# Loading the merge's first rows and weights under the last attention values, and moving a tile's last block behind its other blocks

## The chip, the cores and the metric

The kernel runs on one core of a Trainium2 chip. The metric is the device time of one execution in microseconds (us); a lower time is better. The time shown is the median of three runs; a profile is one further execution.

## What is computed

One layer on 1024 tokens of width 1024, all in float32. A projection of x feeds a short convolution, an attention with three branches (compressed, selected and window) and two gates; the two paths are merged, projected and normalised, and a mixture of 32 experts follows.

```python
y_a = (b_gate * conv) @ w_up_conv
o_nsa = nsa_attention(...)                     # 1024 x 512
y_b = o_nsa @ w_up_nsa                         # 1024 x 1024
merged = sigmoid(mg_a) * y_a + sigmoid(mg_b) * y_b
x1 = layer_norm(DN_ALPHA * x + merged @ w_o, ln1_g, ln1_b)
x2 = layer_norm(DN_ALPHA * x1 + moe_ffn(x1, ...), ln2_g, ln2_b)
```

The change touches the lines of `y_b`, `merged` and `merged @ w_o`.

## The kernel before

**Numbers.** TensorE multiplies in a float32 form of reduced width. So each operand is split into a high part (a cast on ScalarE) and a low part (what is left, a subtraction on VectorE): `split`, lines 110 to 113. A product is three matmuls, high by high, high by low and low by high: `mm3`, lines 116 to 120. Weights too are loaded as float32 and split in this way.

**Order of the work.** The program is written as one sequence for all engines. A scheduler places each engine's instructions, each engine runs its own in the order it was given, and waits are on semaphores. SyncE's queue issues most loads and writes in its order, so an issue that waits holds up those behind it.

**Attention** (`attention`, lines 549 to 708). The work is cut into 16 units: 8 tiles of 128 tokens, and two groups of heads each. `scores(u)` multiplies queries and keys (`s`, L595 and L596), takes the minimum on VectorE (L597) and the exponential on ScalarE (L599). `values(u)` scales the probabilities, transposes them in steps of 128 keys (`t`, L645), splits them (`th`, `tl`, two steps in flight through the two buffers of `t`), and multiplies them into `o` (L638, "flush"). At the end `o` is copied and added (`otmp` L659, `of` L660 and L661) and written to `o_d[0]` (first 512 tokens) or `o_d[1]` (second 512, L662). The values of one unit run beside the scores of the next, so the last unit's values run alone.

**The late projection** (`late`, lines 664 to 685). The gates of the second 512 tokens are projected under the attention: 16 groups of 8 steps, each step one `mm3` from the operands `x[0]` and `x[1]` (tiles `x10`, `x11`) and weights `lw` into `lm`, followed by a tanh `tg` (L680) and a write to `spill` (L684). How fast its 128 steps are handed out beside the scores is a line in `passed`, the work of the scores so far:

```python
while made < 16 * KT * (passed / total * LATE[0] - LATE[1]):   # L696
```

With `LATE = (0.85, -0.05)` (L546) 116 of the 128 steps are handed out by the end of the scores; the rest runs beside and behind the last values.

**Merge** (`merge_route`, from line 762). There are 8 blocks of 128 output columns (`j`) by 2 halves of 512 tokens (`h`). `load_o(h)` (L779) loads and splits the attention's rows of one half, `load(j)` (L787) the up weights of a block, `load_sp(j)` (L795) a block's gates and first path from `spill`. `merge(h, ...)` (L800) is 12 matmuls into one of four PSUM tiles `mm`; then come a join (L805), a sum (L828) and a split into the operands of the next product (`raw` and `m`, L830). `load_wo(j)` (L807) loads and splits a block of `w_o` into `wh` and `wl`.

**Output projection** (`project(i)`, line 895). A tile of 128 tokens is two column halves of 8 blocks, three matmuls each: 48 matmuls. The sum with x (L908) and the layer norm follow. `route`, `place` and `collect` choose the experts' tokens. The experts' stage after it takes some two thirds of the span.

Of the kernel before, what the change touches and what calls it, by code (L numbers as in the profile page):

```python
# [9 lines left out]
F32 = mybir.dt.float32  # L10
F32R = mybir.dt.float32r
# [4 lines left out]
ALU = mybir.AluOpType  # L16
# [106 lines left out]
def pre_phase(nc, tc, io, dbg):  # L123
# [275 lines left out]
    attention(nc, tc, io, ident, gates, q_d, K1, K2, V, K1c, K2c, Vc, o_d, xs[1], w_d, ya_d, spill)  # L399
    elate.close()  # L400
# [17 lines left out]
    routes = merge_route(nc, tc, io, const, dram, left, wp, ident, spill, o_d, x1d, acc, slots, dbg)  # L418
# [127 lines left out]
LATE = (0.85, -0.05)  # L546


def attention(nc, tc, io, ident, gates, q_d, K1, K2, V, K1c, K2c, Vc, o_d, x, w_d, ya_d, spill):
    with ExitStack() as es:  # L550
# [135 lines left out]

        more, made, passed = late(), 0, 0
# [17 lines left out]
        for _ in prev:  # L705
            pass
        for _ in more:
            pass

# [52 lines left out]
def merge_route(nc, tc, io, const, dram, left, wp, ident, spill, o_d, x1d, acc, slots, dbg):  # L762

    with ExitStack() as es:
# [10 lines left out]
        with tc.tile_pool(name="mwo", bufs=1, side="right", reuse_waits="tile") as op, \  # L775
                tc.tile_pool(name="mwa", bufs=2, side="right", reuse_waits="tile") as wk:
            os = []
# [9 lines left out]
            def load(j):  # L787
                wr = wk.tile([P, 4, P], F32, name="wur")
                nc.sync.dma_start(wr, io["wupn"][j])
                wh = wk.tile([P, 4, P], F32R, name="wuh")  # L790
                wl = wk.tile([P, 4, P], F32R, name="wul")
                split(nc, wh, wl, wr)
                return wh, wl

            def load_sp(j):  # L795
                sp = wk.tile([P, 2, T], F32, name="sp")
                nc.sync.dma_start(sp, spill[j])
                return sp

            def merge(h, wh, wl, sp):  # L800
                s = slice(h * 512, h * 512 + 512)
                m = ps.tile([P, 512], F32, name="mm")
                for k in range(4):
                    mm3(nc, m, (wh[:, k], wl[:, k]), (os[h][0][:, k], os[h][1][:, k]), k == 0, k == 3)
                nc.vector.scalar_tensor_tensor(sp[:, 1, s], sp[:, 1, s], 1.0, m, op0=ALU.add, op1=ALU.mult)  # L805
# [8 lines left out]
            load_o(0)  # L814
            us = [load(0)]
            load_o(1)
            us.append(load(1))
            us = [u + (load_sp(j),) for j, u in enumerate(us)]
            for h in range(2):
                for u in us:  # L820
                    merge(h, *u)
            for j in range(KT):
                if j > 1:
                    us.append(load(j) + (load_sp(j),))
                    for h in range(2):
                        merge(h, *us[j])
                sp = us[j][2]
                nc.vector.tensor_tensor(sp[:, 0], sp[:, 0], sp[:, 1], op=ALU.add)  # L828
                for h in range(2):
                    split(nc, *(m[j // 4][:, j % 4] for m in ms[h]), sp[:, 0, h * 512:h * 512 + 512])  # L830
                if j >= WO_LAG:
                    load_wo(j - WO_LAG)
# [62 lines left out]
        def project(i):  # L895
# [4 lines left out]
            nc.scalar.activation(xr, xr, AF.Copy, scale=ALPHA)  # L900
            for h in range(2):
                s = slice(h * 512, h * 512 + 512)
                m = ps.tile([P, 512], F32, name="mm")
                for k in range(KT):
                    c = slice(i % 4 * P, i % 4 * P + P)
                    mm3(nc, m, [v[k // 4][:, k % 4, c] for v in ms[i // 4]], [w[k // 4][h][:, k % 4] for w in wos],
                        k == 0, k == KT - 1)
# [743 lines left out]
```

## Time and profile before

| | |
|---|---|
| median of three runs | 2353.45 us (2350.07 to 2354.51) |
| the profiled execution | 2343.27 us, span 2341.7 us |
| TensorE busy | 2272.9 us, 97% |
| VectorE, ScalarE busy | 1789.1 us (76%), 1420.8 us (61%) |
| last values of the attention end, merge begins | 736.7 us, 750.8 us |
| first output tile begins | 796.4 us |
| data moved | 575.58 MB, mean 246 GB/s |

In the profile PE is TensorE's matmuls, PEld its weight loads, DVE VectorE, ACT ScalarE, POOL GpSimd, SP SyncE; SPq is the queue from which SyncE issues transfers. Matmuls overlap, so the distance between two starts is what one costs, not the duration shown. L805 is line 805 of the kernel. Times in rows count from the start of the span.

### The profile page before, as it was taken

The numbers are of one execution on the slowest core, as the hardware profiler recorded it, in microseconds if no ns is written. First come the engines' busy times: TensorE is split into PE (matmuls) and PEld (weight loads), VectorE is DVE, ScalarE is ACT, GpSimd is POOL, SyncE is SP. The second block draws the span as 40 slices with busy tenths as digits, with TensorE's granted clock in tenths as the row PEclk, the third lists the DMA queues.
The fourth block names the chain that finished last, engine by engine and source line by source line (L and its number), as shares of the span: only waits on it lengthen the run. The fifth ranks groups of instructions, "written<-read, shape, count | busy, mean of one in ns | idle before, by whom it ended". The sixth has DMA issues, their size and how long they took to land. (4 is left out here: it accounts for less than half of the span.)

```text
span 2341.7 us, 35263 instructions
## 1 busy us (share of the span) xinstructions
PE 2272.9 (97%) x12609; PEld 1937.8 (83%) x12611; DVE 1789.1 (76%) x3098; ACT 1420.8 (61%) x2289; POOL 282.2 (12%) x269
## 2 busy tenths in 40 slices
PE   8999999899998999999999999999999999999995
PEld 7888899777886788889898898889898898988972
DVE  4322357697875878888988888989888888989856
ACT  3122245797885412667767767777777777767742
POOL 0000000111110024211101101111111121111000
PEclk9999999999999999999999999999999999999998
DMA  5247434432324833888998889988998889898895
GB/s 186 77 166 264 153 95 126 148 104 64 93 77 144 292 142 121 323 307 291 341 331 313 310 309 314 347 322 299 341 320 323 318 301 352 326 324 321 289 326 233
DMA packets 123419, 575.58 MB, mean 246 GB/s; under 512 B 16969, under 2 KB 27161, under 8 KB 73044
## 3 DMA queue, kind: packets, MB, share of 16 engines
q1 hardware_dynamic: 86192, 475.14, 55.8%
q0 software_dynamic: 20672, 58.80, 9.6%
q10 hardware_dynamic: 16372, 39.32, 4.7%
q8 instruction: 101, 1.65, 0.3%
q14 instruction: 82, 0.67, 0.1%
HBM read 506.08 MB, written 67.50 MB: 245 GB/s over the span
## 5 line engine op out<-in xcount | busy, mean ns | idle before, releaser
L1160 DVE TENSOR_TENSOR wl<-raw,wh 128x1024 fp32r<-128x1024 f32 x744 | 892.5, 1221 | 111.2 <-ACT wh L1159 109.4
L1159 ACT CAST wh<-raw 128x1024 fp32r<-128x1024 f32 x744 | 757.7, 1048 | 296.1 <-PE h L1289 95.1
L1289 PE MATMUL h<-x,wh 128*128 128x288 f32 (+4 forms) x1664 | 420.5, 343 | 0.0
L1290 PE MATMUL h<-x,wl 128*128 128x144 f32 (+4 forms) x1664 | 386.5, 232 | 0.0
L1290 PEld LDWEIGHTS h<-x,wl 128*128 128x128 f32 x1664 | 318.6, 191 | 1.6
L1289 PEld LDWEIGHTS h<-x,wh 128*128 128x128 f32 x1664 | 314.0, 189 | 1.8
L118 PE MATMUL h<-wh,x 128*128 128x512 f32 x576 | 229.9, 399 | 0.0
L119 PE MATMUL h<-wl,x 128*128 128x512 f32 x576 | 227.9, 396 | 0.0
L120 PE MATMUL h<-wh,x 128*128 128x512 f32 x576 | 227.7, 395 | 0.0
L118 PE MATMUL y<-wh,ah 128*128 128x512 f32 x496 | 198.5, 400 | 0.0
L119 PE MATMUL y<-wl,ah 128*128 128x512 f32 x496 | 195.8, 395 | 0.6 <-DVE wl L1160 0.6
L120 PE MATMUL y<-wh,al 128*128 128x512 f32 x496 | 195.7, 395 | 0.0
L1366 POOL DMA_INDIRECT acc<-ysb,ix x31 | 80.1, 2584 | 815.8 <-ACT ysb L1352 815.8
L118 PE MATMUL mm<-x,wh 128*128 128x512 f32 x320 | 126.7, 397 | 7.3 <-ACT x L111 7.3
L120 PEld LDWEIGHTS h<-wh,x 128*128 128x128 f32 x576 | 108.8, 189 | 25.6
L119 PEld LDWEIGHTS h<-wl,x 128*128 128x128 f32 x576 | 108.9, 189 | 24.3
L118 PEld LDWEIGHTS h<-wh,x 128*128 128x128 f32 x576 | 108.9, 189 | 23.2
L120 PE MATMUL mm<-x,wl 128*128 128x512 f32 x320 | 125.9, 393 | 0.0
L119 PE MATMUL mm<-x,wh 128*128 128x512 f32 x320 | 124.7, 390 | 0.0
L112 DVE TENSOR_TENSOR wl<-wr,wh 128x1024 fp32r<-128x1024 f32 (+2 forms) x37 | 40.0, 1081 | 107.3 <-ACT wh L111 107.1
L112 DVE TENSOR_TENSOR tl<-t,th 128x512 fp32r<-128x512 f32 x132 | 90.2, 689 | 36.3 <-ACT th L111 35.2
L120 PEld LDWEIGHTS y<-wh,al 128*128 128x128 f32 x496 | 93.3, 188 | 22.1
(406 smaller groups left out, 4645.2 us busy)
## 6 DMA issues: line engine op xcount, KB each, us to landing
raw<-in_wgu_dram SPq DMA_DIRECT2D x253, 1024.0 KB
raw<-in_wdn_dram SPq DMA_DIRECT2D x127, 1024.0 KB
lw<-w_d POOLq DMA_DIRECT2D x32, 512.0 KB
wr<-in_wmg_dram SPq DMA_DIRECT2D x16, 512.0 KB
w_d<-wh ACTq DMA_DIRECT2D x16, 512.0 KB
w_d<-wl ACTq DMA_DIRECT2D x16, 512.0 KB
sp<-spill SPq DMA_DIRECT2D x8, 1024.0 KB
wr<-in_wconv_dram SPq DMA_DIRECT2D x9, 512.0 KB
```

The source lines that it names most:

```text
L112: nc.vector.tensor_tensor(lo, src, hi.bitcast(F32), op=ALU.subtract)
L118: nc.tensor.matmul(ps, ah, bh, start=first, stop=False)
L119: nc.tensor.matmul(ps, ah, bl, start=False, stop=False)
L120: nc.tensor.matmul(ps, al, bh, start=False, stop=last)
L1159: nc.scalar.copy(w[0][:, a:a + 2], raw[:, a:a + 2])
L1160: ins = nc.vector.tensor_tensor(w[1][:, a:a + 2], raw[:, a:a + 2], w[0][:, a:a + 2].bitcast(F32), op=ALU.subtract)
L1289: nc.tensor.matmul(h[:, gl, :2 * cap], wh[:, k, w], xk, start=not second and k == 0, stop=False)
L1290: nc.tensor.matmul(h[:, gl, :cap], wl[:, k, w], xk[:, 0], start=False, stop=second and k == 3)
L1366: self.nc.gpsimd.indirect_dma_start(out=self.acc, out_offset=bass.IndirectOffsetOnAxis(ap=ix, axis=0), in_=y, in_offset=None, compute_op=A ...
```

## The change

The late projection is handed out faster (0.97), so that it is done before the last scores end. Its operand tiles `x10` and `x11` are then used again: a new generator `early` loads the attention's first 512 tokens into `x10` and the first two blocks of up weights into `x11`, and splits them beside the last values. `merge_route` takes both over. It merges the first tokens of blocks 0 to 3 first, then the second tokens of blocks 0 to 3, then blocks 4 to 7 with both halves. `spill` is loaded by halves (four buffers of half the size), and join, sum and split go by halves. In `project`, the first tile runs blocks 0 to 6 of both column halves before block 7 of either.

```diff
-LATE = (0.85, -0.05)
+LATE = (0.97, -0.05)
...
+        def early():
...
+            o = xl.tile([P, 2, 4, 512], F32R, name="x10")
+            w = xl.tile([P, 4, 2, 512], F32R, name="x11")
+            lo = o[:, 1].bitcast(F32)
+            raws = []
+            for j in range(2):
+                raws.append(wk.tile([P, 512], F32, name="ya"))
+                nc.sync.dma_start(raws[j].rearrange("p (k m) -> p k m", k=4), io["wupn"][j])
+            for c in range(0, 4, 2):
+                nc.sync.dma_start(lo[:, c:c + 2], o_d[0][c:c + 2].rearrange("c p t -> p c t"))
+            for j in range(2):
+                split(nc, w[:, j, 0], w[:, j, 1], raws[j])
+                yield
+            for c in range(0, 4, 2):
+                split(nc, o[:, 0, c:c + 2], o[:, 1, c:c + 2], lo[:, c:c + 2])
+                yield
+            yield o, w
...
-        for _ in prev:
-            pass
         for _ in more:
             pass
+        first = early()
+        for n, _ in enumerate(prev):
+            got = next(first) if n in (4, 6, 8, 10) else None
+        return next(first)
...
-            os = []
+            o0, wus = early
+            os = [[o0[:, 0], o0[:, 1]]]
...
             def load(j):
-                wr = wk.tile([P, 4, P], F32, name="wur")
...
+                wr = wk.tile([P, 512], F32, name="wur")
+                nc.sync.dma_start(wr.rearrange("p (k m) -> p k m", k=4), io["wupn"][j])
+                split(nc, wus[:, j % 4, 0], wus[:, j % 4, 1], wr)
...
+            def load_sp(j, h):
+                sp = wk.tile([P, 2, 512], F32, name="sp", bufs=4)
+                nc.sync.dma_start(sp, spill[j, :, :, h * 512:h * 512 + 512])
                 return sp
...
+            def join(j, h, m, sp):
...
+                nc.vector.scalar_tensor_tensor(sp[:, 1], sp[:, 1], 1.0, m, op0=ALU.add, op1=ALU.mult)
+                nc.vector.tensor_tensor(sp[:, 0], sp[:, 0], sp[:, 1], op=ALU.add)
+                split(nc, *(v[j // 4][:, j % 4] for v in ms[h]), sp[:, 0])
...
-            load_o(0)
-            us = [load(0)]
+            load(2)
+            load(3)
+            sps = [load_sp(0, 0), load_sp(1, 0)]
             load_o(1)
-            us.append(load(1))
-            us = [u + (load_sp(j),) for j, u in enumerate(us)]
-            for h in range(2):
-                for u in us:
-                    merge(h, *u)
+            sps += [load_sp(2, 0), load_sp(3, 0)]
+            part = [merge(j, 0) for j in range(4)]
+            for j in range(4):
+                join(j, 0, part[j], sps[j])
             for j in range(KT):
...
+                if j < 4:
+                    sp = load_sp(j, 1)
+                    join(j, 1, merge(j, 1), sp)
+                else:
+                    load(j)
                     for h in range(2):
...
+                        sp = load_sp(j, h)
+                        join(j, h, merge(j, h), sp)
...
+            part = [ps.tile([P, 512], F32, name="mm") for _ in range(2)]
+
+            for ks in ((range(KT - 1), range(KT - 1, KT)) if i == 0 else (range(KT),)):
+                for h in range(2):
+                    for k in ks:
+                        mm3(nc, part[h], [v[k // 4][:, k % 4, c] for v in ms[i // 4]],
+                            [w[k // 4][h][:, k % 4] for w in wos], k == 0, k == KT - 1)
```

Where instructions move on the engines, at three places. The first is TensorE between the last flushes of the next-to-last unit (`o` from `th` and `tl`) and the first transposes of the last one (`t` from `pc` and `pf`). Before:

```order
L638 MATMUL o_6979<-th_7207,V1_2147 128x512
L118 MATMUL lm_7109<-x10_81,lw0_7103 128x512
L119 MATMUL lm_7109<-x11_82,lw0_7103 128x512
L638 MATMUL o_6979<-tl_7208,V1_2147 128x512
L638 MATMUL o_6979<-th_7218,V1_2147 128x512
L627 MATMUL t_7244<-ident_60,pc_6949 128x128 x2
```

Of the change:

```order
L637 MATMUL o_7041<-th_7256,V1_2147 128x512
L118 MATMUL mm_7542<-x10_7351,x11_7352 128x512
L119 MATMUL mm_7542<-x10_7351,x11_7352 128x512
L120 MATMUL mm_7542<-x10_7351,x11_7352 128x512
L637 MATMUL o_7041<-tl_7257,V1_2147 128x512
L637 MATMUL o_7041<-th_7267,V1_2147 128x512
```

The late matmuls (`lm`) are gone from this place; the merge's first matmuls (`mm` from the attention's rows in `x10` and the up weights in `x11`) stand there, 24 in all before the last unit's transposes are done.

The second place is SyncE's queue around the last writes of the attention's rows (`o_d` from `of`) and of the last gate (`spill` from `tg`). Before:

```order
L684 DMA spill_63<-tg_7418 128x512
L662 DMA o_d1_67<-of_7401 128x2x128
L783 DMA ol0_7504<-o_d0_66 128x2x512
L684 DMA spill_63<-tg_7452 128x512
L783 DMA ol0_7504<-o_d0_66 128x2x512
L783 DMA ol1_7518<-o_d1_67 128x2x512
L789 DMA wur_7511<-in_wupn_dram 128x512
L783 DMA ol1_7518<-o_d1_67 128x2x512
L789 DMA wur_7525<-in_wupn_dram 128x512
L797 DMA sp_7531<-spill_63 128x2048
```

Of the change:

```order
L695 DMA ya_7355<-in_wupn_dram 128x512
L697 DMA x10_7351<-o_d0_66 128x2x512
L683 DMA spill_63<-tg_7168 128x512
L697 DMA x10_7351<-o_d0_66 128x2x512
L661 DMA o_d1_67<-of_7282 128x2x128
L661 DMA o_d1_67<-of_7466 128x2x128
L811 DMA wur_7518<-in_wupn_dram 128x512
L811 DMA wur_7522<-in_wupn_dram 128x512
L816 DMA sp_7526<-spill_63 128x2x512
L816 DMA sp_7528<-spill_63 128x2x512
L805 DMA ol1_7531<-o_d1_67 128x2x512 x2
```

The first tokens' rows and two up weights are now issued ahead of the last two writes of rows; the up weights of blocks 2 and 3 come first behind them, ahead of the second tokens' rows (`ol1`).

The third place is TensorE in the first output tile, at block 7 of the contraction; the two column halves are two tiles `mm`. Before (`mm_7960` is the first half, `mm_7986` the second):

```order
L119 MATMUL mm_7986<-wl_7494,raw_7481 128x512
L118 MATMUL mm_7960<-wh_7491,raw_7482 128x512
L119 MATMUL mm_7960<-wl_7495,raw_7482 128x512
L120 MATMUL mm_7986<-wh_7490,raw_7483 128x512
L120 MATMUL mm_7960<-wh_7491,raw_7484 128x512
L118 MATMUL mm_7986<-wh_7490,raw_7481 128x512
```

Of the change (`mm_7968` and `mm_7969`):

```order
L120 MATMUL mm_7969<-wh_7507,raw_7499 128x512
L118 MATMUL mm_7968<-wh_7506,raw_7497 128x512
L119 MATMUL mm_7968<-wl_7510,raw_7497 128x512
L120 MATMUL mm_7968<-wh_7506,raw_7499 128x512
L118 MATMUL mm_7969<-wh_7507,raw_7497 128x512
L119 MATMUL mm_7969<-wl_7511,raw_7497 128x512
```

Before, the scheduler put five matmuls of the second half ahead of the first half's block 7, so 26 of the tile's 48 stood ahead of it; now 42 do.

## Rows read from the trace of the kernel before

**Rows 1.** The page, busy us (share of the span) and instructions of each engine.
```profile
PE 2272.9 (97%) x12609; PEld 1937.8 (83%) x12611; DVE 1789.1 (76%) x3098; ACT 1420.8 (61%) x2289; POOL 282.2 (12%) x269
```

**Rows 2.** Waits, 735 to 815: who waited for whom: us in total, times, longest.
```profile
PE mm L118 <- ACT wuh L111: 10.1, 1, 10.1
...
PE mm L118 <- ACT raw L111: 2.7, 1, 2.7
```

**Rows 3.** Windows: busy us (xcount) of PE, PEld, DVE, ACT, POOL; PEclk, DMA share, GB/s.
```profile
751.00:755.00 4.00, 4.00 (x11) 3.09 (x12) 2.28 (x3) 1.56 (x2) 0.00 (x0) 0.57 0.98 394
...
805.20:809.20 4.00, 3.98 (x11) 3.11 (x11) 1.29 (x2) 0.49 (x1) 0.00 (x0) 0.57 1.01 345
```

**Rows 4.** Timeline, TensorE, last values: start, us, engine, line, operation.
```profile
733.07 0.39 PE L118 MATMUL lm<-x,lw 128*128 128x512 f32 x1
733.30 0.60 PE L645 MATMUL t<-ident,pw 128*128 128x128 f32 x4
...
734.21 0.62 PE L645 MATMUL t<-ident,pw 128*128 128x128 f32 x4
```

**Rows 5.** Timeline, SyncE's queue, issues after the last values.
```profile
738.26 0.37 SPq L662 DMA_DIRECT2D o_d<-of  x1
740.72 0.37 SPq L783 DMA_DIRECT2D ol<-o_d  x1
...
745.77 0.35 SPq L789 DMA_DIRECT2D wur<-in_wupn_dram  x1
```

**Rows 6.** Timeline, ScalarE, last values and first casts of the merge.
```profile
733.94 0.59 ACT L111 CAST th<-t 128x512 fp32r<-128x512 f32 x1 [0.54 <-PE t L645]
...
736.76 0.58 ACT L659 COPY otmp<-o 64x512 f32<-64x512 f32 x1 [1.31 <-PE o L638]
...
745.11 1.04 ACT L111 CAST oh<-ol 128x1024 fp32r<-128x1024 f32 x1 [3.79 <-DMA ol<-o_d]
...
750.11 0.62 ACT L111 CAST wuh<-wur 128x512 fp32r<-128x512 f32 x1 [0.67 <-DMA wur<-in_wupn_dram]
```

**Rows 7.** Timeline, TensorE, last flush, last late matmul, first merge matmul.
```profile
736.33 0.40 PE L638 MATMUL o<-tl,V 128*128 128x512 f32 x1
...
740.30 0.39 PE L120 MATMUL lm<-x,lw 128*128 128x512 f32 x1
750.78 0.79 PE L118 MATMUL mm<-oh,wuh 128*128 128x512 f32 x1 [10.10 <-ACT wuh L111]
```

**Rows 8.** Timeline, SyncE's queue and VectorE: the last block's spill, join and sum.
```profile
794.61 0.33 SPq L797 DMA_DIRECT2D sp<-spill  x1
...
801.97 1.28 DVE L805 SCALAR_TENSOR_TENSOR sp<-sp,mm 128x512 f32<-128x512 f32 x2 [1.31 <-DMA sp<-spill]
...
803.29 1.22 DVE L828 TENSOR_TENSOR sp<-sp 128x1024 f32<-128x1024 f32 x1
```

**Rows 9.** Timeline, TensorE, block 7 of the first output tile.
```profile
805.22 0.50 PE L118 MATMUL mm<-wh,raw 128*128 128x512 f32 x1 [2.72 <-ACT raw L111]
```

**Rows 10.** Timeline, VectorE, subtractions of the splits.
```profile
733.43 0.69 DVE L112 TENSOR_TENSOR tl<-t,th 128x512 fp32r<-128x512 f32 x1 [0.24 <-ACT th L111]
...
746.19 1.23 DVE L112 TENSOR_TENSOR ol<-ol,oh 128x1024 fp32r<-128x1024 f32 x1 [7.96 <-ACT oh L111]
```

**Rows 11.** Timeline, a 256 KB load on a quiet queue: its issue and the waiting cast.
```profile
322.26 1.69 SPq L297 DMA_DIRECT2D cwr<-in_wq_dram  x3
...
325.37 0.62 ACT L111 CAST cwh<-cwr 128x512 fp32r<-128x512 f32 x1 [1.97 <-DMA cwr<-in_wq_dram]
```

**Rows 12.** Windows in the last scores and in the merge, columns as in rows 3.
```profile
705.90:717.10 11.20, 11.20 (x67) 9.33 (x67) 7.61 (x17) 6.81 (x15) 0.00 (x0) 1.00 0.29 103
780.00:790.00 10.00, 10.00 (x44) 7.93 (x43) 10.00 (x16) 5.53 (x10) 0.00 (x0) 1.00 0.88 316
```

**Rows 13.** Routing: a wait of ScalarE (us, times, longest); TensorE's first transposes of a tile.
```profile
ACT x L900 <- DMA ao<-in_bdn_dram: 5.7, 1, 5.7
...
825.76 1.06 PE L920 MATMUL t<-ident,x 128*128 128x128 f32 x8
```

More of the change, by code (lines that the diff above doesn't have):

```diff
@@ L396, in pre_phase @@
                 pass
-    attention(nc, tc, io, ident, gates, q_d, K1, K2, V, K1c, K2c, Vc, o_d, xs[1], w_d, ya_d, spill)
-    elate.close()
+    early = attention(nc, tc, io, ident, gates, q_d, K1, K2, V, K1c, K2c, Vc, o_d, xs[1], w_d, ya_d, spill, xl)
     if dbg:
@@ L417, in pre_phase @@
     wp = left.enter_context(tc.tile_pool(name="ewp", bufs=WB, reuse_waits="tile"))
-    routes = merge_route(nc, tc, io, const, dram, left, wp, ident, spill, o_d, x1d, acc, slots, dbg)
+    routes = merge_route(nc, tc, io, const, dram, left, wp, ident, spill, o_d, x1d, acc, slots, dbg, early, elate)
     ord_d = dram.tile([1, NE], F32, name="ord_d")
@@ L545, with attention @@
 SCALE_ACT = (0, 2, 2)
-LATE = (0.85, -0.05)
-def attention(nc, tc, io, ident, gates, q_d, K1, K2, V, K1c, K2c, Vc, o_d, x, w_d, ya_d, spill):
+LATE = (0.97, -0.05)
+def attention(nc, tc, io, ident, gates, q_d, K1, K2, V, K1c, K2c, Vc, o_d, x, w_d, ya_d, spill, xl):
     with ExitStack() as es:
@@ L759, with merge_route @@
 WO_LAG = 2
-def merge_route(nc, tc, io, const, dram, left, wp, ident, spill, o_d, x1d, acc, slots, dbg):
+def merge_route(nc, tc, io, const, dram, left, wp, ident, spill, o_d, x1d, acc, slots, dbg, early, elate):
     with ExitStack() as es:
@@ L773, in merge_route @@
         wos = [[[wp.tile([P, 4, 512], F32R, name=n, bufs=WB) for _ in range(2)] for _ in range(2)] for n in ("wh", "wl")]
-        with tc.tile_pool(name="mwo", bufs=1, side="right", reuse_waits="tile") as op, \
+        with elate, tc.tile_pool(name="mwo", bufs=1, side="right", reuse_waits="tile") as op, \
                 tc.tile_pool(name="mwa", bufs=2, side="right", reuse_waits="tile") as wk:
-            os = []
+            o0, wus = early
+            os = [[o0[:, 0], o0[:, 1]]]
             def load_o(h):
@@ L787, in load, with merge @@
             def load(j):
-                wr = wk.tile([P, 4, P], F32, name="wur")
[L789 to L797, printed above, removed]
-                return sp
-            def merge(h, wh, wl, sp):
-                s = slice(h * 512, h * 512 + 512)
+                wr = wk.tile([P, 512], F32, name="wur")
[4 more added lines that the diff above has]
+                nc.sync.dma_start(sp, spill[j, :, :, h * 512:h * 512 + 512])
+                return sp
+            def merge(j, h):
                 m = ps.tile([P, 512], F32, name="mm")
+                wh, wl = (wus[:, j % 4, a].rearrange("p (k m) -> p k m", k=4) for a in range(2))
                 for k in range(4):
                     mm3(nc, m, (wh[:, k], wl[:, k]), (os[h][0][:, k], os[h][1][:, k]), k == 0, k == 3)
-                nc.vector.scalar_tensor_tensor(sp[:, 1, s], sp[:, 1, s], 1.0, m, op0=ALU.add, op1=ALU.mult)
+                return m
+            def join(j, h, m, sp):
+                nc.vector.scalar_tensor_tensor(sp[:, 1], sp[:, 1], 1.0, m, op0=ALU.add, op1=ALU.mult)
+                nc.vector.tensor_tensor(sp[:, 0], sp[:, 0], sp[:, 1], op=ALU.add)
+                split(nc, *(v[j // 4][:, j % 4] for v in ms[h]), sp[:, 0])
             def load_wo(j):
```

15 lines of the change are left out of this document (2 added, 13 removed).

## Prediction, made before the result was known

> **What bounds the kernel now.** I read the page first: TensorE is busy 97% of the span [rows 1], so time is saved only where TensorE idles or runs slow. Next, the list of what TensorE waits for: at the places that the change touches it waited 10.1 us, its longest wait, for a cast of an up weight, and 2.7 us for a cast of the merged rows [rows 2]. Then the stretches right after each: in both, the granted clock is 0.57, a mix of the two levels 1.2 and 2.4 GHz, and 11 matmuls fit into 4.0 us [rows 3]. At full clock one starts every 0.23 us (733.07 to 733.30 in [rows 4]), so 11 take 2.5 us: each wait costs another 1.5 us of slow clock.
>
> The first wait is a chain of transfers. The last late matmul starts at 740.30 [rows 7]; only then is the load of the attention's rows issued (740.72), since it overwrites the late projection's operands; the up weight's is issued at 745.77 [rows 5]. The rows land at 745.11, the weight at 750.11 [rows 6], and TensorE starts at 750.78. The second wait lies inside the first output tile: block 7 of its contraction needs the last merged rows, whose spill was issued at 794.61 and reached VectorE's add at 801.97 [rows 8]; TensorE resumes at 805.22 [rows 9].
>
> **The change, term by term.** The arithmetic stays; I cost positions and queues. The sum is made against the profiled execution, 2343.27 us (span 2341.7), which is 0.4% under the median of the runs shown, 2353.45; I take the difference over to that median.
>
> *Removed at the first wait:* 10.1 + 1.5 = 11.6 us.
>
> *Put in its place.* By the new order blocks 0 and 1 of the first tokens (24 matmuls) run before the last unit's transposes; blocks 2 and 3 follow the last flush and need up weights whose loads stand on SyncE's queue behind the last write of the attention's rows. So a wait is left. From the end of the last flush (736.33 + 0.40 = 736.73 in [rows 7]): copy on ScalarE 0.58 [rows 6], two adds on VectorE, the write's issue 738.26 + 0.37 [rows 5]: the weight's load goes out 1.9 us after the flush. A 256 KB load on a quiet queue took 3.1 us (322.26 to 325.37 in [rows 11]); the same size behind 1.5 MB of others took 4.3 (745.77 in [rows 5] to 750.11 in [rows 6]). The new one is first in line, so I take 3.1 and keep 4.3 for the range. With the cast of 0.62 that is 5.6 us of idle TensorE (6.8 at the far end). The shorter second wait was enough to drop the clock [rows 3], so 1.5 more: 7.1. Net of this place: 11.6 - 7.1 = 4.5 us.
>
> The Trainium skill (DMA: Bandwidth & Descriptors, "Anatomy of one DMA") puts a transfer at 2.0 us plus its bytes at 436 GB/s, an estimate of 2.6 us for this load; with it the wait would be 5.1 and the final sum 6.2 us instead of 5.7. The trace's quiet load is longer, and it is the one used.
>
> *Late matmuls taken out of the last values.* Before, six of them filled gaps there, one per two steps [rows 4]. A step without one takes 0.91 us on TensorE (733.30 to 734.21), two take 1.82; the loop through two buffers is transposes 0.62, cast 0.59, subtraction 0.69 [rows 4, 6, 10], 1.9 us. Nothing now fills the difference: 0.08 us per pair at least, 0.23 (the whole filler) at most, so 0.5 to 1.4 us over six pairs. I take 1.0 lost.
>
> *The early loads and splits.* They wait for the last late matmul, hence the new 0.97 (late projection done before the last scores end). The stretch from there to the first early merge matmul answers to 705.9 to 717.1 before: 11.2 us with TensorE full, ScalarE busy 6.8, VectorE 7.6 [rows 12]. Ten late matmuls of 0.23 lie in it; without them TensorE needs 8.9. ScalarE gets two casts of 0.62 and two of 1.04 [rows 6], 3.3, so 10.1; VectorE two subtractions of 0.69 and one of 1.23 [rows 10], 2.6, so 10.2 (the other 1.23 falls later). They lag TensorE by 1.2 to 1.3. The first half of the rows lands 4.4 us after its issue (740.72 in [rows 5] to 745.11 in [rows 6]); ScalarE is at that cast after about 3.6 (a gate, three casts of 0.59, two of 0.62), so it waits 0.8. Together 2.0 us lost; bounds 0 (the splits spread over earlier slack) and 3. The DMA issues are 0.4 us each on a SyncE queue that is nearly idle in this stretch, so they cost nothing; that cover ends with the last write.
>
> *The second wait.* By the old order 26 matmuls stood between the tile's start and block 7: 5.9 us, plus 2.7 of waiting [rows 9], so its operands came 8.6 us after the start. Now 42 stand ahead, 9.5 us. The wait and its slow clock go: 2.7 + 1.5 = 4.2 us (0 if the last rows come 4 us later than before). What is late next is the normalised first tile, which TensorE transposes at 825.76 with no gap ahead of it [rows 13].
>
> *Edits at nothing:* the joins by halves add 0.16 us of VectorE per block, two adds of 0.69 [rows 10] for one of 1.22 [rows 8], in a stretch where VectorE is full [rows 12]. It runs beside 24 matmuls of TensorE, 5.5 us per block; without that cover it is 1.3 us over eight blocks.
>
> **Sum:** 4.5 - 1.0 - 2.0 + 4.2 = 5.7 us saved; 2353.45 - 5.7 = 2347.8. The experts' stage behind it is bound by TensorE and moves as a whole.
>
> **Rivals.**
> *The DMA engines give it back.* In the merge they are busy 0.88 at 316 GB/s [rows 12]. The change takes 1.5 MB out of this stretch but also shortens it by 8.7 us (4.5 + 4.2), worth 2.75 MB at that rate. The 1.25 MB left over are 4 us: the later up weights, spilled rows, and the biases that the routing stage loads (5.7 us of waiting already, [rows 13]) come late, and TensorE waits before the first tile's transposes. Then 1.7 us are saved: 2351.8. For it: a megabyte took 7.4 us here [rows 8]. Against it: SyncE's queue also waited for buffers, which is no lack of bandwidth. The Trainium skill (DMA: Bandwidth & Descriptors, "Issuing engines are not separate DMA queues") says that transfers of all issuers interleave on the same 16 engines, so moving issues between queues would not help; the row of 0.88 fits it.
>
> *The early rows come too late: slower.* The 24 merge matmuls now stand ahead of the last unit's transposes on TensorE, and the casts of the rows ahead of its last exponentials on ScalarE. If each half took 7.4 us [rows 8], one after the other, the second (issued behind the write of the last gate) would be there at 14.8, split at 17.1; TensorE is there at 8.9: 8.2 idle, 1.5 of clock, and some 3 for the exponentials held back: 12.7 in place of 2.0. That is 5.7 + 2.0 - 12.7 = -5.0: 2358.5. It turns slower once the rows are split some 12 us after the last late matmul. Against it: the engines move 103 GB/s there, 0.29 of their time [rows 12], and half a megabyte took 4.4 us.
>
> That the change does not do what it says I can exclude: the orders show each move.
>
> **How the numbers follow.** Forecast 0.62, DMA 0.25, late rows 0.08; 0.05 for a stall I do not see. Within the forecast the bounds give 8.2 us at best (0.5, 0, 4.2) and about 2.5 at worst with the long load and 3 lost. A difference under 0.2% (4.7 us) can't be told from none by a measurement of this kernel. The forecast is over 4.7 us in most of its cases (0.53 of 0.62), the DMA case in few (0.04): faster 0.57. The rest of both and half of the unseen is 0.34; slower 0.09. The range: 2353.45 - 8.2 and 2 us of scatter (the three runs span 4.4) gives 2343; above, the DMA case with 3 us more, 2355.
>
> **What the changed profile would show.** Right: TensorE's wait after the last flush is 5 to 7 us and ended by a cast of an up weight; two blocks of merge stand ahead of the last unit's transposes without a wait above 1 us; the last scores take about 2 us more with ScalarE near full; no wait at block 7, clock 1.00 through the first tile. Wrong: a long wait of a merge matmul for the early rows; a new wait before the second tokens' blocks or the first tile's transposes; a DMA share near 1 with waits on up weights.

## The result, and the profile after

The changed kernel takes 2362.82 us (median of nine runs, 2359.59 to 2366.80), the kernel before 2350.07 (nine runs, 2343.67 to 2359.80): ratio 1.0051, interval 1.0037 to 1.0066. It is slower by some 12 us; 2347.8 was forecast.

The profile after is of an execution at the median (2362.82); that of before is of an execution below all of its nine (2343.27; their lowest is 2343.67). So the two profiles differ by 19.5 us, not by 12, and 3.4 of them stand already at the first late-projection matmul (420.38 before, 423.83 after), ahead of anything that moved. All stretches below are therefore counted from that matmul, and sizes are taken from the ratios (the times of a kernel's runs over those of the kernel before, taken beside them). The page, busy us and share of the span:

```profile
PE 2285.9 (97%) x12610; PEld 1946.9 (82%) x12611; DVE 1787.1 (76%) x3106; ACT 1421.6 (60%) x2289; POOL 285.1 (12%) x269
```

TensorE's share is what it was [rows 1], with the same work in a longer span: its busy time is 13.0 us longer, with one instruction more. A matmul right behind a wait is shown at 0.79 us where 0.39 is usual (759.37 and 809.49 below). The waits of TensorE from 725 to 870 answer to [rows 2] (us in total, times, longest):

```profile
PE mm L118 <- ACT x L111: 10.0, 2, 5.6
PE t L948 <- DVE rsh L743: 6.1, 1, 6.1
PE mm L120 <- DVE x L112: 1.6, 1, 1.6
PE mm L119 <- DVE ol L112: 0.8, 1, 0.8
```

The two waits of before are gone, and 18.5 us stand in their place. The timeline of TensorE shows where (start, us, engine, line, operation, wait ahead of it); it answers to [rows 7, 9, 13]:

```profile
732.60 0.39 PE L118 MATMUL mm<-x,x 128*128 128x512 f32 x1
...
753.27 0.50 PE L637 MATMUL o<-tl,V 128*128 128x512 f32 x1 [0.18 <-DVE tl L112]
759.37 0.79 PE L118 MATMUL mm<-x,x 128*128 128x512 f32 x1 [5.60 <-ACT x L111]
...
784.17 0.80 PE L118 MATMUL mm<-x,x 128*128 128x512 f32 x1 [4.37 <-ACT x L111]
...
809.49 0.39 PE L118 MATMUL mm<-wh,raw 128*128 128x512 f32 x1
...
840.72 1.94 PE L948 MATMUL t<-ident,x 128*128 128x128 f32 x8 [6.13 <-DVE rsh L743]
```

At 732.60 the early merge matmuls begin, without a wait. At 759.37 is the wait that was forecast at 5.6 us, and it is 5.60. At 784.17, in the middle of the merge, is a wait for an up weight that was not forecast, and at 840.72 one before the first tile's transposes. The first output tile (809.49) now runs without a gap. Each of the three long waits again drags slow clock behind it (windows; columns as in [rows 3]):

```profile
760.00:765.00 5.00, 5.00 (x16) 3.95 (x15) 1.98 (x5) 0.00 (x0) 0.00 (x0) 0.66 1.00 324
...
780.00:785.00 5.00, 0.83 (x2) 0.74 (x3) 4.19 (x8) 2.80 (x5) 0.00 (x0) 0.89 0.95 327
785.00:790.00 5.00, 5.00 (x18) 3.73 (x18) 2.44 (x5) 1.66 (x3) 0.00 (x0) 0.77 1.01 382
...
840.00:850.00 10.00, 9.28 (x34) 8.46 (x35) 4.86 (x17) 1.56 (x4) 0.00 (x0) 0.50 0.21 84
```

From 840 to 850 the granted clock is 0.50, its lower level of 1.2 GHz, and 34 instructions of TensorE fit into these ten us. Before, 58 fit into ten us some way behind the first tile's first transposes (825.76), at full clock:

```profile
830.00:840.00 10.00, 10.00 (x58) 8.27 (x57) 7.62 (x27) 1.81 (x5) 0.00 (x0) 1.00 0.14 54
```

The timelines of ScalarE and of SyncE's queue show what stood ahead of the two new waits:

```profile
782.46 1.14 ACT L111 CAST wh<-wor 128x512 fp32r<-128x512 f32 x2 [1.74 <-DMA wor<-in_wo_dram]
783.50 0.61 ACT L111 CAST x<-wur 128x512 fp32r<-128x512 f32 x1
...
819.57 4.46 ACTq L898 DMA_DIRECT2D ao<-in_bdn_dram  x3
827.85 0.35 ACTq L916 DMA_DIRECT2D places<-in_places_dram  x1
828.25 2.01 ACT L925 ACTIVATE x<-x 128x1024 f32<-128x1024 f32 x2 [14.90 <-DMA x<-in_xn_dram]
```

```profile
755.95 0.82 SPq L811 DMA_DIRECT2D wur<-in_wupn_dram  x2
...
776.32 0.42 SPq L811 DMA_DIRECT2D wur<-in_wupn_dram  x1
...
814.52 14.10 SPq L924 DMA_DIRECT2D x<-in_xn_dram  x8
```

Block 4's up weight is loaded at 776.32 and cast at 783.50, behind two casts of an output weight which no matmul needs before 809 and which had waited for their own transfer. These casts cost little: by the completion records that the trace keeps of each transfer, the up weight landed at 783.11, 0.4 us before its cast. What was late is the issue. TensorE came to block 4 at 779.80 (784.17 less the wait), 3.5 us after it; before, block 4's load went out 12.1 us ahead of its first matmul (774.36):

```profile
762.28 0.33 SPq L789 DMA_DIRECT2D wur<-in_wupn_dram  x1
```

From issue to cast the loads of blocks 4 to 7 took 5 to 9 us in both kernels.

The input rows of the first output tile are issued at 814.52, 5 us after the merge's last matmul; before, at 798.06, 1.8 us after it (796.22). But these rows are not what came last. The first of them had landed at 822.97 by the completion records, and ScalarE scaled it at 828.25 (L925), because its own queue (ACTq) had loads of biases (L898) and of `places` (L916) to issue ahead of that, and the issues wait for earlier loads to land. The wait of 14.90 us in the row, put down to an input row, ends with the last of these issues, at 828.20.

Three stretches of TensorE hold nearly all of it: A from the first late-projection matmul to the 25th merge matmul (the first of block 2 in the new order), B on to the first matmul of the first output tile, C on to the experts' first matmul. In us, from the start times in each timeline, with the ratio to the kernel before:

| kernel | A | B | C | ratio (95% interval) |
|---|---|---|---|---|
| before | 337.7 | 38.4 | 142.1 | 1 |
| after | 335.5 | 50.1 | 149.6 | 1.0051 (1.0037 to 1.0066) |
| late97 | 345.5 | 38.4 | 140.9 | 1.0037 (1.0024 to 1.0050) |
| last7 | 339.2 | 39.2 | 146.5 | 1.0021 (1.0010 to 1.0033) |
| late85 | 330.2 | 49.6 | 145.6 | 1.0022 (1.0011 to 1.0034) |
| up_ahead | 336.3 | 42.1 | 146.2 | 1.0008 (0.9995 to 1.0020) |
| up_pool | 336.4 | 50.0 | 145.9 | 1.0049 (1.0033 to 1.0064) |
| first_loads_pool | 331.5 | 55.2 | 146.2 | 1.0037 (1.0023 to 1.0051) |
| adds_pool | 335.1 | 56.9 | 148.7 | 1.0088 (1.0068 to 1.0109) |
| x_rows_moved | 336.3 | 49.6 | 144.0 | 1.0042 (1.0025 to 1.0058) |
| no_last7 | 336.4 | 49.1 | 143.4 | 1.0052 (1.0034 to 1.0071) |
| all_mended | 316.6 | 61.1 | 144.1 | 1.0008 (0.9995 to 1.0021) |
| up_ahead_no_last7 | 336.4 | 41.4 | 144.4 | 1.0009 (0.9997 to 1.0020) |
| up_ahead_no_last7_late85 | 330.0 | 41.5 | 147.5 | 0.9986 (0.9974 to 0.9998) |
| best_wo_pool | 331.5 | 40.0 | 148.8 | 0.9985 (0.9974 to 0.9995) |
| best_wo_pool_moved | 334.8 | 40.4 | 149.2 | 0.9981 (0.9971 to 0.9991) |
| x_rows_turned | 336.6 | 51.6 | 147.3 | 1.0053 (1.0033 to 1.0072) |

So A became 2.2 us shorter, B 11.7 and C 7.5 longer; that is 17.0 in all where the ratio says 12. A single profile's stretches scatter by some us: no_last7 has a C 6 us under that of after and the same ratio, and best_wo_pool and best_wo_pool_moved, which do the same work up to the end of A, differ there by 3.3. So A and C are read with care.

### The profile page after: what moved, and what is told of

The parts are those of the page before. It is cut to its first block, busy times and chain, and to the rows that moved or that the text cites. A ratio compares the mean times of both kernels' runs of the same rounds, so it can differ in the third digit from the quotient of the medians.

```text
span 2361.2 us, 35296 instructions
## 1 busy us (share of the span) xinstructions
PE 2285.9 (97%) x12610; PEld 1946.9 (82%) x12611; DVE 1787.1 (76%) x3106; ACT 1421.6 (60%) x2289; POOL 285.1 (12%) x269
## 5 line engine op out<-in xcount | busy, mean ns | idle before, releaser
L112 DVE TENSOR_TENSOR tl<-t,th 128x512 fp32r<-128x512 f32 x132 | 89.5, 688 | 49.6 <-ACT th L111 49.0
```

The costliest lines, as they stand in the source:

```text
L112: nc.vector.tensor_tensor(lo, src, hi.bitcast(F32), op=ALU.subtract)
```

## The experiments

**1. One part of the change alone, on the kernel before.** late97, where last7 takes over the new `project`:

```diff
-LATE = (0.85, -0.05)
+LATE = (0.97, -0.05)
```

> The kernel before with the late projection's constant alone at 0.97 in place of 0.85: some 16 of its steps less are left for after the last values. Theory 'the last values had room for them': the steps put 3.9 us of matmuls per 16 into the stretch before, and the gaps of the last values (waits for VectorE's tl) stay empty, so the last flush comes 3 to 5 us later, with as much less after it; ratio 0.9990 to 1.0015, a change of under 1 us either way at the merge's first matmul. Rival 'the fuller stretch costs more than it brings': the merge's first matmul comes 4 us or more later than 750.78 plus what the late projection's start differs, ratio 1.0015 to 1.003.

late97: ratio 1.0037, some 8.7 us slower; the rival has the direction right, and the cost is above its range (up to 1.003). The profiles differ in A (+7.8), hardly elsewhere. Its windows:

```profile
440.00:460.00 20.00, 17.89 (x101) 14.62 (x101) 17.56 (x63) 19.68 (x70) 2.12 (x4) 0.93 0.36 112
730.00:740.00 10.00, 6.06 (x23) 3.71 (x23) 7.86 (x15) 7.63 (x14) 0.00 (x0) 0.69 0.14 34
740.00:750.00 10.00, 9.20 (x47) 7.30 (x46) 5.86 (x8) 5.32 (x9) 0.00 (x0) 0.80 0.09 33
```

Between the last scores and the last values TensorE waits for the softmax, and with the late projection used up (its last matmul is at 720.47) nothing fills that hole: 6.06 of 10 us busy, clock 0.69 and 0.80. Before, late matmuls ran there, until 740.30 [rows 7]. Without them the wait at the merge's first matmul is 5.49 us in place of 10.10, and A is longer all the same. A smaller loss stands in the first units (17.89 busy of 20 from 440 to 460, 19.58 before).

> The kernel before with the first output tile's order alone changed: its block 7 comes last. The forecast said 2.7 us of wait and 1.5 of clock go, 4.2 in all: ratio 0.9982, 2342.5 us beside 2346.7. Rival 'what follows waits instead': the first tile's norm is bound by its input rows (first addition at 812.49) and not by TensorE, TensorE's wait goes from block 7 to the first transposes, under 1.5 us of gain: ratio 0.9993 to 1.0005.

```diff
-    for h in range(2):
-        for k in range(KT):
+    for ks in ((range(KT - 1), range(KT - 1, KT)) if i == 0 else (range(KT),)):
+        for h in range(2):
+            for k in ks:
```

last7: 1.0021; neither expectation, it is slower. The wait for block 7 went and came back before the transposes, larger, with the clock at 0.57 behind it:

```profile
831.35 1.94 PE L923 MATMUL t<-ident,x 128*128 128x128 f32 x8 [4.55 <-DVE bmv L745]
```

```profile
830.00:840.00 10.00, 8.65 (x33) 7.93 (x34) 5.80 (x20) 1.56 (x4) 0.00 (x0) 0.57 0.13 52
```

The first tile's norm begins with ScalarE's scaling of the first input row (L900), and that waits for ScalarE's own queue. Before, and in last7:

```profile
806.04 4.84 ACTq L873 DMA_DIRECT2D ao<-in_bdn_dram  x3
...
811.40 1.06 ACT L900 ACTIVATE x<-x 128x1024 f32<-128x1024 f32 x1 [5.71 <-DMA ao<-in_bdn_dram]
```

```profile
812.23 4.77 ACTq L873 DMA_DIRECT2D ao<-in_bdn_dram  x3
...
817.52 2.12 ACT L900 ACTIVATE x<-x 128x1024 f32<-128x1024 f32 x2 [6.01 <-DMA ao<-in_bdn_dram]
```

By the completion records the row itself had landed at 805.93 and 811.53, 5.5 and 6.0 us before it was scaled; between, ScalarE issued the three loads of the biases, which wait for earlier loads to land. So the norm comes when that queue is through, and a TensorE that doesn't wait at block 7 waits there. No run moves these issues, so what they are worth is not measured.

**2. One part undone in the changed kernel.** late85:

```diff
-LATE = (0.97, -0.05)
+LATE = (0.85, -0.05)
```

no_last7:

```diff
-    for ks in ((range(KT - 1), range(KT - 1, KT)) if i == 0 else (range(KT),)):
+    for ks in (range(KT),):
```

> The changed kernel with the late projection's constant back at 0.85, the rest of the change kept: the 16 steps left over (48 matmuls, 11 us) run after the last scores and before the last values, where late97 leaves TensorE idle (6.06 of 730 to 740) and its clock at 0.69; the early loads, whose buffers the late projection reads, come after them. Theory 'those steps are the cover of that gap': the ratio falls by most of what late97 lost (0.0037), to 1.001 to 1.003. Rival 'the early merge matmuls are as good a cover' (9.95 of 730 to 740 are busy in the changed kernel): no gain, and the first merge matmuls come later, 1.004 to 1.007.

late85: 1.0022, and the intervals of 1.0051 and 1.0022 don't overlap: some 7 us came from the constant. A falls by 5.3. From 430 to 750 TensorE waits 7.2 us in all in place of 8.8, and after the last flush 3.02 in place of 5.60, since the late steps fill the hole and the early merge matmuls are left for the last values and for that wait:

```profile
730.88 0.39 PE L120 MATMUL lm<-x,lw 128*128 128x512 f32 x1
...
747.10 0.43 PE L637 MATMUL o<-tl,V 128*128 128x512 f32 x1
747.37 0.39 PE L119 MATMUL mm<-x,x 128*128 128x512 f32 x1
...
753.04 0.50 PE L118 MATMUL mm<-x,x 128*128 128x512 f32 x1 [3.02 <-ACT x L111]
```

> The changed kernel with the first output tile in its old order (all eight blocks of one half, then of the other). If the new order costs as much here as alone on the kernel before (last7: 1.0021), the ratio goes from 1.0051 to about 1.003, 2355 us beside 2348. Theory of the forecast (the new order saves a wait for block 7): the ratio rises to 1.006 or more. Third: the first tile waits for its input rows either way (first load at 814.5), no difference, 1.0045 to 1.0057.

no_last7: 1.0052, no difference: the third theory's number. In the changed kernel the first tile's norm comes so late that the order of the tile costs and brings nothing. What is late is again ScalarE's queue, and not the input rows that the expectation names: the first row landed at 821.76 and was scaled at 826.06.

**3. The wait inside the merge.** up_ahead moves one call:

```diff
                 if j < 4:
                     sp = load_sp(j, 1)
-                    join(j, 1, merge(j, 1), sp)
+                    m = merge(j, 1)
+                    load(j + 4)
+                    join(j, 1, m, sp)
                 else:
-                    load(j)
```

> The up weights of blocks 4 to 7 are loaded and split one step earlier each (block j+4's right after block j's last matmul), ahead of spilled rows and output weights in SyncE's queue. Theory 'the order of SyncE's loads sets the merge': the waits of 4.37 and 1.59 us and the slow clock of 780 to 790 go, 2355.5 us, 2354 to 2358. Rival 'VectorE sets it': the waits on TensorE go, or turn into waits for VectorE, and the last split still ends at 813 to 815: 2361 to 2364 us.

up_ahead: 1.0008, some 10 us less, the largest single piece. B falls from 50.1 to 42.1, and the last split ends at 807.45, so VectorE did not set the end at 814.5, as the rival had it. What it takes from the output weights shows in the first tile, where TensorE now waits 3.1 and 2.6 us for them:

```profile
PE mm L118 <- ACT wh L111: 3.1, 2, 1.8
...
PE mm L119 <- DVE wl L112: 2.6, 1, 2.6
```

adds_pool tests VectorE from the other side:

```diff
-    nc.vector.tensor_tensor(sp[:, 0], sp[:, 0], sp[:, 1], op=ALU.add)
+    nc.gpsimd.tensor_tensor(sp[:, 0], sp[:, 0], sp[:, 1], op=ALU.add)
```

> The merge's 16 additions (0.69 us each on VectorE, 11 us in all) are done by GpSimd (1.3 us each by its rows in the attention stage), everything else as it is. Theory 'VectorE sets the merge's length': the last split ends 6 to 10 us before 814.5: 2354 us, 2351 to 2358. Rival 'the order of SyncE's loads sets it' (TensorE waits 4.37 and 1.59 us for up weights in 780 to 800): these waits stay and the end moves by under 2 us, 2361 to 2364 us.

adds_pool: 1.0088, slower than the changed kernel, with 11 us of additions taken off VectorE. An addition takes 1.45 us on GpSimd (0.69 on VectorE), and the sixteen joins are a chain: the next spilled half may be loaded only when a join has freed its buffer. SyncE's queue waits for that (load L816, us in total, times, longest) 32.5 us there, where in the changed kernel it was 19.9 (12.2 and 7.7):

```profile
SPq L816 <- DVE raw L112: 20.2, 6, 8.2
SPq L816 <- DVE m L112: 12.3, 6, 3.1
```

This speaks for the joins' latency as the pace, and against VectorE's sum. It does not settle it, since VectorE was disturbed as well: the six of its 40 subtractions that began during one of GpSimd's additions took 1.10 to 1.78 us, and all 40 took 33.1 us in place of 28.5. For the low halves of the output weights, first the changed kernel, then adds_pool (count | us in all, mean ns | idle before):

```profile
L112 DVE TENSOR_TENSOR wl<-wor,wh 128x512 fp32r<-128x512 f32 x16 | 10.6, 686 | 3.3 <-ACT wh L111 3.3
```

```profile
L112 DVE TENSOR_TENSOR wl<-wor,wh 128x512 fp32r<-128x512 f32 x12 | 11.1, 956 | 0.0
```

up_pool changes the issuer alone (`load` passes it to its transfer):

```diff
-    load(j)
+    load(j, nc.gpsimd)
```

> The changed kernel, where the up weights of blocks 4 to 7 are issued by GpSimd and not by SyncE; the program's order of loads, splits, matmuls and joins is left as it is (up_ahead had changed that too). Theory 'SyncE's queue': the waits of 4.37 and 1.59 us go as with up_ahead, ratio 1.000 to 1.003 in place of 1.0051. Rival 'the place of the splits on ScalarE and VectorE': the loads land early and the casts still come behind those of the output weights, waits of 3 us or more stay: 1.004 to 1.006.

up_pool: 1.0049, so the queue alone is not it. The loads of blocks 4 and 5 go out at 758.27 and 758.89 (776.32 and 781.08 in the changed kernel), the wait of 4.37 is gone, and TensorE waits 3.07 us for the low half of block 5's up weight, until 789.65. VectorE's timeline:

```profile
786.49 0.69 DVE L112 TENSOR_TENSOR wl<-wor,wh 128x512 fp32r<-128x512 f32 x1 [0.70 <-ACT wh L111]
...
788.90 0.69 DVE L112 TENSOR_TENSOR x<-wur,x 128x512 fp32r<-128x512 f32 x1
```

The up weight's split at 788.90 stands behind an output weight's at 786.49, which had waited in its turn. What counts is the place of load and both halves of the split in three in-order queues together: SyncE's, ScalarE's and VectorE's. up_ahead moved all of them.

**4. The loads after the last flush.** first_loads_pool:

```diff
-    load(2)
-    load(3)
-    sps = [load_sp(0, 0), load_sp(1, 0)]
+    load(2, nc.gpsimd)
+    load(3, nc.gpsimd)
+    sps = [load_sp(j, 0, nc.gpsimd) for j in range(4)]
     load_o(1)
-    sps += [load_sp(2, 0), load_sp(3, 0)]
```

> The up weights of blocks 2 and 3 and the four first spilled halves are issued by GpSimd, so that they don't stand behind SyncE's last store of the attention rows (which goes out at 755.95). Theory 'VectorE sets the merge's length' (its joins run from 763.66 to 814.5 with under 6 us idle): the first join starts at about 757, the last split ends at about 808, and TensorE's 5.60 us wait after the last flush falls under 2 us: 2356 us, 2354 to 2359. Rival 'TensorE sets it': the wait of 5.6 with 1.5 of clock goes, the joins follow TensorE, 2355.5 us, but the last split's end moves by what TensorE's waits give and not by what the first join's start gives. Rival 'transfers set it': the later loads come as much later as these come earlier, 2361 to 2364 us.

first_loads_pool: 1.0037; A is 4.0 shorter and B 5.1 longer: the wait after the flush fell to 1.19, and one of 5.97 came for the next up weight at 766.05. The ratio is at the upper edge of the first expectation and can't be told from 1.0051. The first expectation's wait came, its joins did not: the first is at 769.09 and not at 757, and the last split ends at 814.55, as in the changed kernel. By the stretches it is the third: what was loaded earlier, something else got later.

**5. The input rows.** x_rows_turned makes the eight tiles first and uses them in turned order (`xr = xrs[(i + 1) % NT]`). It was meant to place the first input rows over other buffers, and they got the old address (first load at 815.58, behind the last split; ratio 1.0053); it shows nothing.

> The eight tiles of the first output's input rows are dealt in turned order, so that the first ones lie over the second tokens' attention rows (last read by the merge's last matmul) and not over the merge's spilled rows (last read by VectorE's last split at 814.5). Theory 'place in memory': the first load of them goes out at about 809.5 instead of 814.52, the first tile's norm ends some 5 us earlier, TensorE's 6.13 us wait before the first tile's transposes falls under 2 us and its slow clock (0.71 in 830 to 850) mostly goes: 2355 us, 2353 to 2358. Rival 'transfers are the limit there' (DMA share 1.0 in 820 to 830): the rows land as late as now, wait of 4 us or more, 2361 to 2364 us.

x_rows_moved does it, since the first tile that is written takes the buffer over the spilled rows:

```diff
+    xrs = [wk.tile([P, D], F32, name="x1", bufs=NT) for _ in range(NT)]
+    nc.gpsimd.memset(xrs[NT - 1][:, 0:1], 0.0)
...
-    xr = wk.tile([P, D], F32, name="x1", bufs=NT)
+    xr = xrs[i]
```

> The changed kernel, with the eight tiles of the first output's input rows shifted by one buffer: a one-column memset takes the buffer that lies over the spilled rows' for the last tile, and the first tile lies over the second tokens' attention rows. (The earlier kernel x_rows_turned was meant to do that and didn't: its first load still went out at 815.58, behind the last split.) Theory 'place in memory': the first load goes out when the merge's last matmul ends (about 809.5), 5 us earlier; the 6.1 us wait before the first transposes falls to 1 to 2 us: ratio to the kernel before about 1.002 in place of 1.005, 2351 to 2355 us beside 2346.7 of before. Rival 'transfers are the limit': unchanged wait, 1.0045 to 1.0055.

```profile
837.65 1.27 PE L950 MATMUL t<-ident,x 128*128 128x128 f32 x8 [3.51 <-DVE rsh L743]
```

The first load goes out at 809.01, and the wait falls from 6.13 to 3.51. The place in memory is shown to hold the load back. That the first tile waited for this load is not: the row landed at 813.68, and ScalarE scaled it 8 us later, when its queue was through the loads of the biases:

```profile
815.94 5.25 ACTq L898 DMA_DIRECT2D ao<-in_bdn_dram  x3
...
821.76 2.01 ACT L927 ACTIVATE x<-x 128x1024 f32<-128x1024 f32 x2 [8.10 <-DMA tokid<-in_tokid_dram]
```

Then VectorE waits another 4.03 us for a cast of these biases, which stands in its queue ahead of the rest of the first tile's norm. The ratio of 1.0042 can't be told from 1.0051; the edit's worth here, 2 us by these two, is not clear of nothing.

**6. Together.** all_mended has up_ahead, x_rows_moved, and in `early`:

```diff
+    for j in range(2, 4):
+        raws.append(wk.tile([P, 512], F32, name="tg"))
+        nc.sync.dma_start(raws[j].rearrange("p (k m) -> p k m", k=4), io["wupn"][j])
...
+    for j in range(2, 4):
+        split(nc, w[:, j, 0], w[:, j, 1], raws[j])
```

> The changed kernel with three edits: the up weights of blocks 2 and 3 are loaded during the last values too and split right after them; those of blocks 4 to 7 one step ahead; the input rows moved as in x_rows_moved. Theory 'each wait is one of place in a queue or in memory': from up_ahead (ratio 1.0008) another 5.6 us with 1.5 of clock go after the last flush, and 3 to 5 us before the first transposes: ratio 0.996 to 0.998, 2337 to 2342 us beside 2346.7. Rival 'spilled rows and VectorE set the merge': the joins still begin at about 763 when the first spilled rows land, the last split still ends at 806 to 807, ratio 0.9995 to 1.001.

all_mended: 1.0008, as up_ahead alone. That is the rival's number, with its signs: the joins begin at 762.90 and the last split ends at 807.74. So it is not excluded that spilled rows and VectorE set the merge's pace once the up weights come early. The wait of 5.6 is gone, and TensorE waits 8.60 at the next thing:

```profile
767.40 1.22 PE L118 MATMUL mm<-oh,x 128*128 128x512 f32 x2 [8.60 <-ACT oh L111]
```

These are the second tokens' rows, which exist only after the last flush and its store. A and B together are 377.7 here and 378.4 with up_ahead. Loading the weights earlier moved the wait after the last flush on. late85, which keeps merge matmuls of the first tokens back for it, is the kernel that shortened it (3.02).

The next two kernels hold the edits that their names list.

> Both: up weights of blocks 4 to 7 one step ahead, and the first output tile in its old order. If the two parts add up: 1.0051 - 0.0043 - 0.0021 = 0.9987, 2345 us beside 2348. If with the up weights ahead the output weights are what the first tile waits for (their last split ends at 819.4 there), the old order stalls earlier at those and gains nothing: 1.0005 to 1.0015.

up_ahead_no_last7: 1.0009, as up_ahead; the first tile waits for output weights now.

> All three edits, the best that the parts allow: 0.9987 if the constant makes no difference here; 0.996 to 0.998 (2339 to 2343 us beside 2348) if the steps as cover are worth 2 to 6 us; 1.001 or more if the early loads come too late.

up_ahead_no_last7_late85: 0.9986 (0.9974 to 0.9998), 2344.97 us beside 2347.80, a little faster than both kernels. The number is that of the case "the constant makes no difference", but by luck: beside up_ahead_no_last7 (1.0009) the constant is worth 5 us, and the old order of the tile, which that sum had counted at 5, brought nothing. A and B are 371.5 in place of 376.1 before: 4.6 us saved. By the profile C gives all of that back (147.5 for 142.1), with waits of 4.2 and 3.8 us for output weights; by the ratio some 3 us are left.

best_wo_pool adds to that:

```diff
-    nc.sync.dma_start(wr, io["wo"][j // 2, :, j % 2])
+    nc.gpsimd.dma_start(wr, io["wo"][j // 2, :, j % 2])
```

> up_ahead_no_last7_late85 (0.9986) with the output weights issued by GpSimd instead of SyncE, where they stand behind spilled rows: there TensorE waits 4.2 and 3.8 us for them in the first output tile, at a clock of 0.83 in 810 to 820. Theory 'SyncE's queue': their last split ends at about 803 and not 813.8, these waits go: 0.994 to 0.9965, 2334 to 2340 us beside 2348. Rival 'transfers are the limit' (DMA share 0.83 to 0.94 from 770 to 820): spilled rows come as much later as the output weights come earlier, the merge's waits return: 0.998 to 1.000.

best_wo_pool: 0.9985 (0.9974 to 0.9995), nothing gained, and TensorE still waits 4.3 and 3.4 us for output weights. GpSimd's issues of them wait for the two staging buffers, which a split has to free:

```profile
805.47 0.53 POOL L834 DMA_DIRECT2D wor<-in_wo_dram  x1 [5.80 <-DVE wl L112]
```

So the rival's time came, by another cause than it named. The wait after the last flush is 5.5 us again (3.1 in the kernel that it builds on); why is not shown.

best_wo_pool_moved adds the edit of x_rows_moved.

> best_wo_pool with the input rows moved as in x_rows_moved, so that their first load doesn't wait for the last split. If the first tile's norm is bound by its input rows: another 2 to 3 us, 0.993 to 0.9955. If those rows are limited by transfers: as best_wo_pool within 0.001.

best_wo_pool_moved: 0.9981 (0.9971 to 0.9991), not to be told from best_wo_pool. The first input row goes out at 796.63, 11.6 us earlier; the first tile waits for output weights.

## Why the prediction was wrong

Per stretch, the forecast's terms were: A -3.0 (11.6 - 5.6 off, 1.0 and 2.0 on), B +1.5 (the slow clock after the new wait), C -4.2. Profiled: -2.2, +11.7, +7.5. So two steps failed: B had no term for what stands behind block 3, and C's 4.2 us, counted as a gain, did not come.

*The first wait: right, and to the hundredth by luck.* 5.6 us forecast, 5.60 measured, ended by the cast of an up weight; clock 0.66 behind it. The weight's load went out 2.2 us after the flush (1.9 forecast) and its cast began 2.75 us later (3.1 forecast): two misses of 0.3 that cancel. The 2.6 us that the prediction set beside its 3.1, by the Trainium skill (DMA: Bandwidth & Descriptors, "Anatomy of one DMA"), were nearer; the page gives that fit for transfers that GpSimd issues, and this one was issued by SyncE. The early rows came in time (no wait at 732.60), so the rival of late rows fell.

*"Hence the new 0.97": costed too low.* I counted 3.0 us for it and the early loads, because the late matmuls leave the last scores and values, and not that they had covered the hole before the last values. By late85 the constant costs some 7 us here, by late97 8.7 alone. The early merge matmuls fill that hole in its place (9.95 us busy from 730 to 740), and are then missing later. So A is 2.2 shorter where 330.2, 7.5 shorter, was to be had. It did not break the sum, since A came out within 1 us of its forecast.

*The merge from block 2 on: no term at all, 10 us.* "I cost positions and queues", but only as far as block 3. The loads and splits of blocks 4 to 7 had moved as well, behind spilled rows and output weights: block 4's went out 3.5 us ahead of TensorE in place of 12.1. *Edits at nothing* priced the joins by halves on VectorE alone. On SyncE's queue they are twelve waits for a join's buffer where there had been six, no longer in sum (19.9 us, 20.4 before); but block 4's load, which stood ahead of all of them, now stands behind four. Before, none of the 192 merge matmuls waited after the first. This is the step that turned the sign: up_ahead, which moves four loads and their splits and nothing else, takes back 10 of the 12 us.

*"The wait and its slow clock go: 4.2 us": wrong.* last7 alone costs 4.9 us. The text named the normalised first tile as late next, and left its price at zero because the transposes had no gap ahead of them [rows 13]. They had none because TensorE had already waited, for 2.72 us [rows 9]: the two waits were one slack in two places. The row that told it stood there too: ScalarE's scaling waited 5.7 us behind the biases' loads [rows 13], which the prediction names in its DMA rival alone.

*The DMA rival had the places right* (later up weights, then the first tile's transposes) *and the size wrong:* it gave back 4 us of 5.7. Its cause is not shown, and the runs speak against it: the engines moved 289 GB/s in B of the changed kernel and 300 in B of up_ahead, which is 8 us shorter, so they were not at their limit in the 50.1 us. Moving issues between engines left the time where it was (up_pool, best_wo_pool), and moving the order of load and split did not. The Trainium skill (DMA: Bandwidth & Descriptors, "Issuing engines are not separate DMA queues") says that transfers of all issuers share the same 16 engines. up_pool's 1.0049 and best_wo_pool's 0.9985 beside 0.9986 agree with it, though in both the trace shows a wait for a split or a buffer.

Redone, one bound of the prediction is off: the worst case with the long load and 3 us lost adds up to 3.1 us saved and not 2.5, with the 4.2 us of the second wait still in it, though the text gives 0 as that term's bound.

The parts do not simply add: late97 and last7 alone sum to 13.6 us, the whole change costs 12, while undoing last7 in it brings nothing and up_ahead brings 10. That each part hides behind the next is what the runs show. Left open: how much of C's last 5 us in the best version is the output weights' staging buffers, since no kernel had more of them, and what ScalarE's issues ahead of the first scaling cost, since no kernel moved them.

## What to carry to other kernels

A wait that goes has to be followed to the next thing that arrives late: the same slack can stand in two places, and taking it away in the first moves it to the second, with slow clock on top. When the order of a stage is rewritten, trace every load and split in it to its new place in each in-order queue, to the stage's end, and not only at the waits that were to be removed: what is needed last must not stand ahead of what is needed now. Before a late tile is put down to its own load, see what else stood in the queue of the engine that uses it first. And filler work has a place where it is worth most; spending it early leaves a hole where nothing else can run.

## What was not expected of the hardware

The same 128x512 addition of 0.69 us on VectorE took 1.45 on GpSimd in the merge and 1.31 in the attention stage, and being off VectorE did not help. VectorE's subtractions that began during such an addition took 1.10 to 1.78 us, and 0.69 otherwise. A load's issue that waits holds up the engine's own work: ScalarE scaled an input row 5.5 us after it had landed, behind issues of other loads. The slow clock behind the 6.13 us wait before the first transposes lasted longer (0.50 from 840 to 850, 0.89 from 850 to 860) than behind the 4.37 us wait in the merge (0.77 from 785 to 790); whether the longer wait or the smaller matmuls behind it did that, no run separates.
